# S5 output side: scan states brought into operand layout by a ScalarE copy and a round trip through DRAM, in place of VectorE and TensorE transposes

## The chip, the cores and the metric

The kernel runs on one core of one Trainium2 chip. The metric is the time of one execution on the device in microseconds; the time before is the median of three runs. TensorE (PE) multiplies matrices, VectorE (DVE) and ScalarE (ACT) do elementwise work and evacuate PSUM, GpSimd (POOL) does a little elementwise work and issues some DMAs, SyncE (SP) issues most DMAs. The 16 DMA engines of the core serve all queues.

## What is computed

Two layers on a sequence of 256 frames with 2048 channels: a gated linear attention layer (GLA) and an S5 layer, each with a modulation by a conditioning vector, a gate path and a layer norm around it. The change lies in the S5 layer, in the output side of its state space model. Cut to what matters:

```python
proj = u_in @ w_in                                  # 2048 -> 2 x 4096
u, z = jnp.split(proj, 2, axis=-1)
# 256 groups of 16 channels, 64 complex states each
bu = einsum('blgi,gpi->blgp', u_b, b)               # input side
x  = associative_scan(lam * x_prev + bu)            # over the 256 frames
y  = einsum('blgp,gip->blgi', x_r, c_re) - einsum('blgp,gip->blgi', x_i, c_im)
y  = gelu(y + d_skip * u)
y  = y * sigmoid(y @ w_glu + b_glu)
y  = (y * silu(z)) @ w_out
```

All matrices are float32; the large products are computed as three products of float32r halves (high x high, low x high, high x low), so every weight tile is split into `hi` (a ScalarE cast) and `lo` (a VectorE subtraction).

## The kernel before

Time is laid out in stages, each a loop over weight tiles of 512 KB: `v`, `q` and `z` of the GLA layer, its output product, then for S5 `su` (u), `sz` (z), `gl` (the GLU product) and the output product. A weight tile is loaded by SP (`wload`, line 136), split (`split`, lines 145 and 146) and multiplied (`st_step`, lines 180 to 182, 24 matmuls a step). The other work runs beside it: closures wait in a list `bg`, and after each weight step `pump(rate)` takes out as many as the rate says, in the order of the list. What is emitted is put in program order on each engine's queue; each engine works through its queue in order.

The S5 sequence is cut into 32 blocks of 8 frames. The state enters each block by a scan over the blocks, done on VectorE (`scan`, lines 1188 to 1190, half of the groups at a time) in the tile `sx` (partition; half, block c, part r, group n). The output of the 8 frames of a block is then, for each f (8 groups, f = 0 to 31), the sum of a product of the inputs `U` with a Toeplitz kernel `mt` and of the states at the block's start with C times the powers of lambda (`wc`).

The `sz` stage has 8 groups g of 8 weight steps. Group 0 finishes the input side. Then the list `bg` is filled with the output side, which runs beside groups 1 to 7 (56 steps) at `Y_RATE` items a step. For f = 0 to 33 the list holds:

- three scan steps of the second half of the groups, as long as there are any (30 in all, so in the first ten f);
- `cside(f)`: `cload(f + 1)` (lines 1221 and 1223: one DMA of C and powers, two of the C with its halves swapped) and `mload(f)` (line 1237), both on SP, and `cunit(f)`, the two VectorE products of lines 1070 and 1071 that make `wc`;
- `xstage(f - 1)`: the states of f are transposed by VectorE in 32 x 32 blocks out of `sx` (line 1245, tile `xT`), then by TensorE with the identity (line 1248, two transposes into PSUM, `psxs`), and copied by ScalarE to `xS` (line 1250);
- `ystage(f - 2)`: the matmuls with `mt` (line 1260) and with `xs` and `wc` (line 1263) into `psy`, a VectorE transpose (line 1266, `yt`) and the gelu on ScalarE (line 1267), which writes back into `U`.

The 126 items at 2.311 a step end within the 56 steps. `dma` is a DMA issued by SP, `wdma` one issued by GpSimd. The DRAM tile `rec` holds for each f and partition the rows C, powers of lambda and B that `cload`, `bload` (lines 1050 and 1052) and `kload` (line 1060) read; it is written by GpSimd's DMAs in the preparation (lines 613 and 628), which runs beside the GLA layer. After each group, ScalarE applies the SiLU to `sz` (line 1290).

Of the kernel before, what the change touches and what calls it, by code (L numbers as in the profile page):

```python
# [8 lines left out]
F32 = mybir.dt.float32  # L9
# [6 lines left out]
P = 128  # L16
D = 2048
E = 4096
T = 256
# [14 lines left out]
def trunk(ctx, tc, x, c, ln_g, ln_b, ada_w, ada_b, gla_w_in, gla_gate_w2, gla_gate_b, gla_norm_g,  # L34
# [3 lines left out]
    V, S, PE = nc.vector, nc.scalar, nc.tensor  # L38
# [32 lines left out]
    tp = Phase()  # L71
# [8 lines left out]
    def psx(name):  # L80
        return ax.tile([P, 512], F32, tag="ax", name=name)
# [377 lines left out]

    rec = dp.tile([P, 32, 384], F32, name="rec")

    dk = dp.tile([512, 1920], F32, name="dk")
    dxn = dp.tile([T, D], F32, name="dxn")

    l8 = cp.tile([P, 2, 2, 2, 64], F32, name="l8")
    dT = cp.tile([16, 256], F32, name="dT")
# [129 lines left out]
    def prep_pow(t):  # L598

        pw = SM["pw"]  # L600
        pd = s8t(f"pd{t}", [8, 2, 2, 64])
        for h in range(2):
            S.copy(pd[:, :, :, h, :], pw[:, :, :, t * 64:t * 64 + 64])
        lc = s8t(f"lc{t}", [16, 2, 8, 8])
        for ri in range(2):
            for nb in range(2):
                ps = psx(f"pspw{t}{ri}{nb}")
                for i in range(4):
                    n = nb * 4 + i
                    PE.transpose(ps[:, i * P:(i + 1) * P], pd[:, n, ri].rearrange("g h p -> g (h p)"), ident)  # L610
                pv = ps.rearrange("p (n f g) -> p n f g", n=4, f=16)
                S.activation(lc[:, :, ri, :, nb * 4:nb * 4 + 4].rearrange("p f g n -> p n f g"), pv, AF.Identity, scale=sgn if ri else 1.0)
        wdma(rec[:, 16 * t:16 * t + 16, 128:256], lc.rearrange("p f r g n -> p f (r g n)"))

    def to_rows(src, i_of, t, o, nm):
        got = {}

        def step(ib):
            if ib == 0:
                got["a"] = s8t("rows" + nm, [128, 16])  # L620
            a = got["a"]
            ps = psx(f"psr{nm}{ib}")
            for i in range(4):
                PE.transpose(ps[:, i * P:(i + 1) * P], i_of(src(), 4 * ib + i), ident)
            S.copy(a[:, :, 4 * ib:4 * ib + 4].rearrange("p g i -> p i g"), ps.rearrange("p (i g) -> p i g", i=4))
            if ib == 3:
                av = a.rearrange("p (f g) i -> p f (g i)", f=16)
                wdma(rec[:, 16 * t:16 * t + 16, o:o + 128], av)

        return [lambda ib=ib: step(ib) for ib in range(4)]  # L630

    def prep_b(t):
        got = {}

        def load():
            bi = s8t(f"bin{t}", [2, 64, 16])
            got["bi"] = bi
            dma(bi[:, 0], s5_b_re[0, t * P:(t + 1) * P])
            dma(bi[:, 1], s5_b_im[0, t * P:(t + 1) * P])

        def comp():
            bi = got["bi"]
            bb = s8t(f"bb{t}", [2, 64, 16])
            tm = s8t(f"bt{t}", [64, 16])
            cr = SM["cr"][:, t * 64:t * 64 + 64].unsqueeze(2).to_broadcast([P, 64, 16])
            ci = SM["ci"][:, t * 64:t * 64 + 64].unsqueeze(2).to_broadcast([P, 64, 16])
            V.tensor_tensor(bb[:, 0], bi[:, 0], cr, op=ALU.mult)
            V.tensor_tensor(tm, bi[:, 1], ci, op=ALU.mult)
            V.tensor_tensor(bb[:, 0], bb[:, 0], tm, op=ALU.subtract)
            V.tensor_tensor(bb[:, 1], bi[:, 1], cr, op=ALU.mult)  # L650
            V.tensor_tensor(tm, bi[:, 0], ci, op=ALU.mult)
            V.tensor_tensor(bb[:, 1], bb[:, 1], tm, op=ALU.add)
            got["b"] = bb.rearrange("g r p i -> g (r p) i")

        return [load], [comp] + to_rows(lambda: got["b"], lambda s, i: s[:, :, i], t, 256, f"b{t}")

    def prep_c(t):
        got = {}

        def load():  # L660
            ci = s8t(f"cin{t}", [2, 16, 64])
            got["ci"] = ci
            dma(ci[:, 0], s5_c_re[0, t * P:(t + 1) * P])
            dma(ci[:, 1], s5_c_im[0, t * P:(t + 1) * P])

        def comp():
            ci = got["ci"]
            cc = s8t(f"cc{t}", [16, 2, 64])
            S.copy(cc[:, :, 0, :], ci[:, 0])
            S.mul(cc[:, :, 1, :], ci[:, 1], -1.0)  # L670
            got["c"] = cc

        return [load], [comp] + to_rows(lambda: got["c"], lambda s, i: s[:, i].rearrange("g r p -> g (r p)"), t, 0, f"c{t}")

    (lb0, cb0), (lc0, cc0), (lb1, cb1), (lc1, cc1) = prep_b(0), prep_c(0), prep_b(1), prep_c(1)
    lam = prep_lambda()
# [9 lines left out]
    KEEP = (4, 6)  # L686
    GATE_AT = 20
    SCAN_RATE = 1.728
    Y_RATE = 2.311
    qt, kt = qk  # L690
    gl = {}

# [354 lines left out]
    def bload(f2):  # L1047

        a = tp.tile([P, 2, 384], F32, tag="rb", name=f"rb{f2}", bufs=2)
        dma(a[:, :, 0:256], rec[:, 2 * f2:2 * f2 + 2, 128:384])  # L1050
        for h in range(2):
            dma(a[64 * h:64 * h + 64, :, 256:384], rec[64 - 64 * h:128 - 64 * h, 2 * f2:2 * f2 + 2, 256:384])
        rb[f2] = a

    rc = {}
# [1 line left out]
    def kload(f2):  # L1057

        a = rc[f2] = tp.tile([P, 2, 144], F32, tag="rc", name=f"rc{f2}", bufs=2)
        dma(a, rec[:, 2 * f2:2 * f2 + 2, 0:144])  # L1060

    wb = {}

    def powmul(o, t, a0, a1, l):

        n = o.shape[2]
        bc = lambda z: z.rearrange("p (g i) -> p g i", g=8).unsqueeze(2).to_broadcast([P, 8, n, 16])
        lv = l.rearrange("p (r g n) -> p r g n", r=2, g=8)
        lq = lambda r: lv[:, r, :, :n].unsqueeze(3).to_broadcast([P, 8, n, 16])
        V.tensor_tensor(o, bc(a0), lq(0), op=ALU.mult)  # L1070
        V.tensor_tensor(t, bc(a1), lq(1), op=ALU.mult)
# [146 lines left out]

    def cload(f):
        a = tp.tile([P, 384], F32, tag="cl", name=f"cl{f}", bufs=2)  # L1220
        dma(a[:, 0:256], rec[:, f, 0:256])
        for h in range(2):
            dma(a[64 * h:64 * h + 64, 256:384], rec[64 - 64 * h:128 - 64 * h, f, 0:128])
        cl[f] = a

    def cunit(f):
        a = cl[f]
        w = [tp.tile([P, 8, 8, 16], F32, tag=f"wc{i}", name=f"wc{i}{f}", bufs=2) for i in range(2)]
        powmul(w[0], w[1], a[:, 0:128], a[:, 256:384], a[:, 128:256])
        wc[f] = w  # L1230

    kap = dk[:, :]
# [6 lines left out]

    xss = {}  # L1240

    def xstage(f):
        xt_ = tp.tile([P, 2, 4, 32], F32, tag="xt", name=f"xT{f}", bufs=1)
        n = 2 * (f % 16)
        V.transpose(xt_, sx[:, f // 16, 0:32, :, n:n + 2].rearrange("p c r b -> p b r c"))
        px = psx(f"psxs{f}")
        for b in range(2):
            PE.transpose(px[:, b * P:(b + 1) * P], xt_[:, b].rearrange("p r l -> p (r l)"), ident)
        xs = tp.tile([P, 2, 128], F32, tag="xs", name=f"xS{f}", bufs=2)
        S.copy(xs, px[:, :T].rearrange("p (b r) -> p b r", b=2))  # L1250
        xss[f] = xs

    def ystage(f):
        xs = xss[f]
        py = psx(f"psy{f}")
        U = Ut[f // 8][:, f % 8]
        for b in range(2):
            o = py[:, b * P:(b + 1) * P]
            for q in range(4):
                PE.matmul(o[32 * q:32 * q + 32], lhsT=U[:, b, 32 * q:32 * q + 32], rhs=mt[f][:, :, 2 * q + b, :], start=True, stop=False)  # L1260
            for w in wc[f]:
                for q in range(4):
                    PE.matmul(o[32 * q:32 * q + 32], lhsT=xs[:, b, 32 * q:32 * q + 32],
                              rhs=w[:, 2 * q + b].rearrange("p n i -> p (n i)"), start=False, stop=(w is wc[f][-1]))
        yt = tp.tile([P, 8, 32], F32, tag="yt", name=f"yt{f}", bufs=2)
        V.transpose(yt, py[:, :T].rearrange("p (b t i) -> p t b i", b=2, t=8))
        S.activation(U, yt.rearrange("p t c -> p (t c)").rearrange("p (b r) -> p b r", b=2), AF.Gelu_apprx_tanh)

# [7 lines left out]
    for g in range(8):  # L1276
# [14 lines left out]
        if g == 0:  # L1291
            bstep(len(bq))
            while bg:
                bg.pop(0)()
            less(mid)
            tp.close()
            tp.open("tmp2")
            cload(0)
            sc1 = [lambda cidx=cidx: scan(cidx, 1) for cidx in range(1, 31)]
            for f in range(34):  # L1300
                for _ in range(3):
                    if sc1:
                        bg.append(sc1.pop(0))
                if f < 32:
                    bg.append(lambda f=f: cside(f))
                if 1 <= f < 33:
                    bg.append(lambda f=f: xstage(f - 1))
                if f >= 2:
                    bg.append(lambda f=f: ystage(f - 2))
    while bg:  # L1310
# [149 lines left out]
```

## Time and profile before

| | us |
|---|---|
| three runs | 1847.47 (median), 1845.74, 1847.80 |
| profiled execution, first to last instruction (its span) | 1844.7 |
| `sz` beside the output side (first matmul of group 1 to the first of `gl`) | 1067.5 to 1296.3 |
| busy TensorE, VectorE, ScalarE, GpSimd over the span | 1795.5, 1422.5, 897.4, 72.7 |

For the profiled execution the span is listed and no device time of its own; the median of the runs is 2.8 us above that span. The page divides the span into 40 slices and gives each engine's busy share in tenths. "PEld" is the loading of weights into TensorE, which overlaps its matmuls. The share of DMA is that of the 16 DMA engines together. In the groups, the columns are line, engine, operation, output and input tiles, count, then busy time and mean duration in ns, then the idle time just before and what ended it. The chain of waits is the work that ended last, followed back from the end; a piece of it shows where the time itself went.

### The profile page before, as it was taken

The numbers are of one execution on the slowest core, as the hardware profiler recorded it, in microseconds if no ns is written. First come the engines' busy times: TensorE is split into PE (matmuls) and PEld (weight loads), VectorE is DVE, ScalarE is ACT, GpSimd is POOL, SyncE is SP. The second block draws the span as 40 slices with busy tenths as digits, with TensorE's granted clock in tenths as the row PEclk, the third lists the DMA queues.
The fourth block names the chain that finished last, engine by engine and source line by source line (L and its number), as shares of the span: only waits on it lengthen the run. The fifth ranks groups of instructions, "written<-read, shape, count | busy, mean of one in ns | idle before, by whom it ended". The sixth has DMA issues, their size and how long they took to land.

```text
span 1844.7 us, 33886 instructions
## 1 busy us (share of the span) xinstructions
PE 1795.5 (97%) x13619; PEld 1588.5 (86%) x13619; DVE 1422.5 (77%) x1890; ACT 897.4 (49%) x1252; POOL 72.7 (4%) x78
## 2 busy tenths in 40 slices
PE   7999999999999999999999999999999999999997
PEld 5776897899999888899999999988888888888885
DVE  4877657879989888697899689888677775557556
ACT  5433557556556333654454454545544444444332
POOL 0000000000000000002223200000000000000000
PEclk9999999999999999999999999999999999999999
DMA  9996875889889998465654477899688886668653
GB/s 343 386 333 248 294 244 164 279 261 325 291 286 317 333 353 281 163 220 158 183 151 147 139 214 222 235 246 238 224 276 264 276 271 206 191 189 325 194 184 92
DMA packets 243798, 449.48 MB, mean 244 GB/s; under 512 B 19572, under 2 KB 48942, under 8 KB 242358
## 3 DMA queue, kind: packets, MB, share of 16 engines
q1 hardware_dynamic: 239320, 436.02, 73.9%
q0 software_dynamic: 3552, 10.24, 1.8%
q8 instruction: 107, 1.75, 0.4%
q10 hardware_dynamic: 768, 1.05, 0.2%
q14 instruction: 51, 0.42, 0.1%
HBM read 432.81 MB, written 14.42 MB: 242 GB/s over the span
## 4 chain that ended last, share of the span: by engine, by line
PE 86%; DVE 8%; DMA 3%; ACT 2%; issue 2%; SPq 0%; DVEq 0%; ACTq 0%
PE gl L192 13%; PE gl L193 7%; PE op L168 6%; PE op L167 6%; PE op L169 6%; PE z L182 3%; PE z L180 3%; PE z L181 3%; PE sz L180 3%; PE v L168 3%; PE v L169 3%; PE sz L181 3%; PE sz L182 3%; PE v L167 3%; PE su L180 2%; PE su L182 2%
## 5 line engine op out<-in xcount | busy, mean ns | idle before, releaser
L146 DVE TENSOR_TENSOR logl<-wgl,higl 128x1024 fp32r<-128x1024 f32 x128 | 156.5, 1224 | 115.3 <-ACT higl L145 113.7
L145 ACT CAST higl<-wgl 128x1024 fp32r<-128x1024 f32 x128 | 134.4, 1051 | 172.2 <-PE gl L192 167.9
L192 PE MATMUL gl<-yb,higl 128*128 128x512 f32 x512 | 179.6, 395 | 0.0
L192 PE MATMUL gl<-yp,higl 128*128 128x512 f32 x512 | 179.3, 395 | 0.1
L145 ACT CAST hio<-wo 128x1024 fp32r<-128x1024 f32 x95 | 100.2, 1055 | 155.3 <-PE op L169 127.3
L146 DVE TENSOR_TENSOR loo<-wo,hio 128x1024 fp32r<-128x1024 f32 x95 | 116.2, 1225 | 67.2 <-ACT hio L145 63.7
L315 DVE SCALAR_TENSOR_TENSOR acc<-wa,cs,acc 128x512 f32<-128x512 f32 x217 | 162.2, 748 | 4.8 <-DMA wa<-in_ada_w 2.1
L180 PE MATMUL su<-u1h,hisu 128*128 128x256 f32 x512 | 153.5, 301 | 1.9 <-DVE vv L1108 1.9
L180 PE MATMUL sz<-u1h,hisz 128*128 128x256 f32 x512 | 149.7, 292 | 1.2 <-ACT zs L1290 1.2
L180 PE MATMUL z<-u0h,hiz 128*128 128x256 f32 x512 | 148.7, 290 | 0.0
L182 PE MATMUL su<-u1h,losu 128*128 128x256 f32 x512 | 145.7, 286 | 0.4 <-DVE losu L146 0.4
L181 PE MATMUL su<-u1l,hisu 128*128 128x256 f32 x512 | 145.8, 285 | 0.0
L182 PE MATMUL z<-u0h,loz 128*128 128x256 f32 x512 | 144.9, 283 | 0.6 <-DVE loz L146 0.6
L182 PE MATMUL sz<-u1h,losz 128*128 128x256 f32 x512 | 144.9, 283 | 0.0
L181 PE MATMUL sz<-u1l,hisz 128*128 128x256 f32 x512 | 144.7, 283 | 0.0
L181 PE MATMUL z<-u0l,hiz 128*128 128x256 f32 x512 | 144.7, 283 | 0.0
L193 PE MATMUL gl<-yb,logl 128*128 128x256 f32 x512 | 143.4, 280 | 0.0
L193 PE MATMUL gl<-yp,logl 128*128 128x256 f32 x512 | 142.0, 280 | 0.0
L145 ACT CAST hisz<-wsz 128x1024 fp32r<-128x1024 f32 x64 | 66.9, 1051 | 107.2 <-PE sz L181 55.1
L192 PEld LDWEIGHTS gl<-yb,higl 128*128 128x128 f32 x512 | 96.0, 188 | 22.6
L192 PEld LDWEIGHTS gl<-yp,higl 128*128 128x128 f32 x512 | 95.8, 188 | 22.6 <-issue 0.6
L145 ACT CAST hisu<-wsu 128x1024 fp32r<-128x1024 f32 x64 | 66.7, 1050 | 95.1 <-PE su L181 70.6
(322 smaller groups left out, 5019.8 us busy)
## 6 DMA issues: line engine op xcount, KB each, us to landing
wgl<-in_s_w_glu SPq DMA_DIRECT2D x128, 512.0 KB, 4.7
wa<-in_ada_w SPq DMA_DIRECT2D x116, 512.0 KB, 5.1
wv<-in_gla_w_in SPq DMA_DIRECT2D x64, 512.0 KB, 6.1
wz<-in_gla_w_in SPq DMA_DIRECT2D x64, 512.0 KB, 5.2
wsu<-in_s_w_in SPq DMA_DIRECT2D x64, 512.0 KB, 3.7
wsz<-in_s_w_in SPq DMA_DIRECT2D x64, 512.0 KB, 4.3
wo<-in_s_w_out SPq DMA_DIRECT2D x64, 512.0 KB, 4.5
a<-in_ada_w SPq DMA_DIRECT2D x31, 1024.0 KB, 10.7
```

The source lines that it names most:

```text
L145: S.copy(hi, w)
L146: last_lo[0] = V.tensor_tensor(lo, w, hi.bitcast(F32), op=ALU.subtract).ins
L167: PE.matmul(banks[tt], lhsT=uh, rhs=hi[:, kk, :], start=(k == first), stop=False)
L168: PE.matmul(banks[tt], lhsT=uh, rhs=lo[:, kk, :], start=False, stop=False)
L169: last_mm[0] = PE.matmul(banks[tt], lhsT=ul, rhs=hi[:, kk, :], start=False, stop=(k == last)).ins
L180: PE.matmul(o, lhsT=wh, rhs=u.hi(k), start=(k == first), stop=False)
L181: PE.matmul(o, lhsT=wh, rhs=u.lo(k), start=False, stop=False)
L182: last_mm[0] = PE.matmul(o, lhsT=wl, rhs=u.hi(k), start=False, stop=(k == last)).ins
L192: PE.matmul(banks[f], lhsT=hi[:, kk, fs], rhs=u.both(k), start=(k == 0), stop=False)
L193: PE.matmul(banks[f][:, :T], lhsT=lo[:, kk, fs], rhs=u.hi(k), start=False, stop=(k == last))
L315: V.scalar_tensor_tensor(acc[0], w[:, kk, :], cs[:, k:k + 1], acc[0], op0=ALU.mult, op1=ALU.add)
```

## The change

- `xstage` is replaced by two functions. `xwrite(f)` lets ScalarE copy the states of f out of `sx` into a dense tile `xt_` (one buffer) in the order part r, group b, block c, and GpSimd's queue writes it as 128 rows of 1 KB to a new DRAM tile `dx`. `xread(f)` reads them back on the same queue so that the partitions hold (state l, part r) and the free axis the quarter q: 512 pieces of 256 B. `xs` has three buffers.
- The partitions of `xs` are now in another order, (l r) in place of (r l), and `wc` must have the same. `cload` therefore reads its rows in that order, and in one DMA of 1536 B a row: `rec` is widened to 512 and also holds C with its halves swapped, which two further GpSimd DMAs for each half of the groups write in the preparation. Offsets in `bload` and `kload` move along.
- The lhsT of line 1263 is `xs[:, q, b]`.
- `yt` has one buffer in place of two.
- In the list, `xwrite(f + 1)` (for f = 0 also `xwrite(0)`) and `xread(f)` stand between `cside(f)` and `ystage(f - 2)`. The list has 158 items, and `Y_RATE` is 2.9.

```diff
-    rec = dp.tile([P, 32, 384], F32, name="rec")
+    rec = dp.tile([P, 32, 512], F32, name="rec")
+    dx = dp.tile([32, P, 256], F32, name="dx")
...
                 wdma(rec[:, 16 * t:16 * t + 16, o:o + 128], av)
+                if o == 128:
+                    for h in range(2):
+                        wdma(rec[64 * h:64 * h + 64, 16 * t:16 * t + 16, 0:128], av[64 - 64 * h:128 - 64 * h])
...
-    Y_RATE = 2.311
+    Y_RATE = 2.9
...
     def cload(f):
         a = tp.tile([P, 384], F32, tag="cl", name=f"cl{f}", bufs=2)
-        dma(a[:, 0:256], rec[:, f, 0:256])
-        for h in range(2):
-            dma(a[64 * h:64 * h + 64, 256:384], rec[64 - 64 * h:128 - 64 * h, f, 0:128])
+        dma(a, rec[:, f, 0:384].rearrange("(r l) x -> l r x", r=4))
         cl[f] = a
...
-        powmul(w[0], w[1], a[:, 0:128], a[:, 256:384], a[:, 128:256])
+        powmul(w[0], w[1], a[:, 128:256], a[:, 0:128], a[:, 256:384])
...
-    def xstage(f):
-        xt_ = tp.tile([P, 2, 4, 32], F32, tag="xt", name=f"xT{f}", bufs=1)
+    def xwrite(f):
+        xt_ = tp.tile([P, 4, 2, 32], F32, tag="xt", name=f"xT{f}", bufs=1)
         n = 2 * (f % 16)
-        V.transpose(xt_, sx[:, f // 16, 0:32, :, n:n + 2].rearrange("p c r b -> p b r c"))
-        px = psx(f"psxs{f}")
-        for b in range(2):
-            PE.transpose(px[:, b * P:(b + 1) * P], xt_[:, b].rearrange("p r l -> p (r l)"), ident)
-        xs = tp.tile([P, 2, 128], F32, tag="xs", name=f"xS{f}", bufs=2)
-        S.copy(xs, px[:, :T].rearrange("p (b r) -> p b r", b=2))
-        xss[f] = xs
+        S.copy(xt_, sx[:, f // 16, 0:32, :, n:n + 2].rearrange("p c r b -> p r b c"))
+        wdma(dx[f], xt_.rearrange("p r b c -> p (r b c)"))
+
+    def xread(f):
+        xs = xss[f] = tp.tile([P, 4, 2, 32], F32, tag="xs", name=f"xS{f}", bufs=3)
+        wdma(xs.rearrange("p q b c -> p q (b c)"), dx[f].rearrange("(q l) (r x) -> (l r) q x", q=4, r=4))
...
-                    PE.matmul(o[32 * q:32 * q + 32], lhsT=xs[:, b, 32 * q:32 * q + 32],
+                    PE.matmul(o[32 * q:32 * q + 32], lhsT=xs[:, q, b],
...
-        yt = tp.tile([P, 8, 32], F32, tag="yt", name=f"yt{f}", bufs=2)
+        yt = tp.tile([P, 8, 32], F32, tag="yt", name=f"yt{f}", bufs=1)
...
-                if 1 <= f < 33:
-                    bg.append(lambda f=f: xstage(f - 1))
+                for i in range(0 if f == 0 else f + 1, min(f + 2, 32)):
+                    bg.append(lambda i=i: xwrite(i))
+                if f < 32:
+                    bg.append(lambda f=f: xread(f))
                 if f >= 2:
                     bg.append(lambda f=f: ystage(f - 2))
```

More of the change, by code (lines that the diff above doesn't have):

```diff
@@ L612, in prep_pow @@
                 S.activation(lc[:, :, ri, :, nb * 4:nb * 4 + 4].rearrange("p f g n -> p n f g"), pv, AF.Identity, scale=sgn if ri else 1.0)
-        wdma(rec[:, 16 * t:16 * t + 16, 128:256], lc.rearrange("p f r g n -> p f (r g n)"))
+        wdma(rec[:, 16 * t:16 * t + 16, 256:384], lc.rearrange("p f r g n -> p f (r g n)"))
     def to_rows(src, i_of, t, o, nm):
@@ L653, in comp @@
             got["b"] = bb.rearrange("g r p i -> g (r p) i")
-        return [load], [comp] + to_rows(lambda: got["b"], lambda s, i: s[:, :, i], t, 256, f"b{t}")
+        return [load], [comp] + to_rows(lambda: got["b"], lambda s, i: s[:, :, i], t, 384, f"b{t}")
     def prep_c(t):
@@ L671, in comp @@
             got["c"] = cc
-        return [load], [comp] + to_rows(lambda: got["c"], lambda s, i: s[:, i].rearrange("g r p -> g (r p)"), t, 0, f"c{t}")
+        return [load], [comp] + to_rows(lambda: got["c"], lambda s, i: s[:, i].rearrange("g r p -> g (r p)"), t, 128, f"c{t}")
     (lb0, cb0), (lc0, cc0), (lb1, cb1), (lc1, cc1) = prep_b(0), prep_c(0), prep_b(1), prep_c(1)
@@ L1049, in bload @@
         a = tp.tile([P, 2, 384], F32, tag="rb", name=f"rb{f2}", bufs=2)
-        dma(a[:, :, 0:256], rec[:, 2 * f2:2 * f2 + 2, 128:384])
+        dma(a[:, :, 0:256], rec[:, 2 * f2:2 * f2 + 2, 256:512])
         for h in range(2):
-            dma(a[64 * h:64 * h + 64, :, 256:384], rec[64 - 64 * h:128 - 64 * h, 2 * f2:2 * f2 + 2, 256:384])
+            dma(a[64 * h:64 * h + 64, :, 256:384], rec[64 - 64 * h:128 - 64 * h, 2 * f2:2 * f2 + 2, 384:512])
         rb[f2] = a
@@ L1059, in kload @@
         a = rc[f2] = tp.tile([P, 2, 144], F32, tag="rc", name=f"rc{f2}", bufs=2)
-        dma(a, rec[:, 2 * f2:2 * f2 + 2, 0:144])
+        dma(a, rec[:, 2 * f2:2 * f2 + 2, 128:272])
     wb = {}
```

## The prediction

> **What bounds the kernel now.** I read the page first, then the engines' busy time in stretches, then the stretch that the change touches by its groups, its chain of waits, its waits and its DMA.
>
> ```profile
> PE 1795.5 (97%) x13619; PEld 1588.5 (86%) x13619; DVE 1422.5 (77%) x1890; ACT 897.4 (49%) x1252; POOL 72.7 (4%) x78
> DMA  9996875889889998465654477899688886668653
> ```
>
> Over the whole span TensorE is the bound, but the DMA digits rise to 9 in places. The edited code runs in the seven groups of `sz` that follow group 0, from 1067.5 us to the first `gl` matmul at 1296.3 us. By stretches (columns: length, then busy time of PE, PEld, DVE, ACT, POOL, granted clock, DMA share, GB/s):
>
> ```profile
> 1067.50:1152.50 85.00, 83.76 (x939) 80.91 (x938) 81.25 (x148) 40.94 (x59) 0.00 (x0) 1.00 0.78 223
> 1152.50:1210.00 57.50, 57.13 (x824) 53.44 (x823) 50.35 (x55) 29.37 (x47) 0.00 (x0) 1.00 0.91 241
> 1210.00:1265.00 55.00, 50.89 (x733) 47.20 (x731) 44.40 (x48) 28.11 (x43) 0.00 (x0) 1.00 1.00 238
> 1265.00:1290.00 25.00, 24.26 (x375) 22.49 (x376) 23.47 (x30) 14.25 (x27) 0.00 (x0) 1.00 0.98 247
> 1290.00:1296.30 6.30, 6.30 (x88) 5.95 (x87) 6.30 (x12) 5.93 (x9) 0.00 (x0) 1.00 0.37 107
> 1067.50:1296.30 228.80, 222.33 (x2951) 209.99 (x2950) 205.78 (x288) 118.60 (x182) 0.00 (x0) 1.00 0.88 230
> 1296.30:1664.00 367.70, 367.63 (x2088) 320.31 (x2087) 243.29 (x289) 178.05 (x227) 0.00 (x0) 1.00 0.75 241
> ```
>
> The stage has two halves. In the first 85 us (the scan of the second half runs beside it) VectorE is nearly as full as TensorE and the DMA engines are free 22% of the time. From 1152.5 us on there is no scan, so more f pass per weight step, and DMA is at 0.91, 1.00 and 0.98. The groups of the stretch (from 1066 to 1300 us) that the change names, and steps of the chain of waits (start, length):
>
> ```profile
> L1245 DVE STREAM_TRANSPOSE xT<-sx 128x256 f32<-128x256 f32 x32 | 20.1, 627 | 1.2 <-PE psxs L1248 0.9
> L1248 PE MATMUL psxs<-ident,xT 128*128 128x128 f32 x64 | 12.3, 274 | 1.2 <-DVE xT L1245 1.2
> L1250 ACT COPY xS<-psxs 128x256 f32<-128x256 f32 x32 | 11.5, 361 | 2.0 <-PE psxs L1248 2.0
> L1267 ACT ACTIVATE U<-yt 128x256 f32<-128x256 f32 x32 | 13.3, 416 | 6.5 <-DVE yt L1266 6.4
> ```
> ```profile
> 1060.11 0.12 PE sz L182
> ...
> 1123.61 0.39 ACT zs L1290
> ...
> 1182.11 0.22 PE psxs L1248 x2
> 1182.33 0.36 PE psy L1260 x8
> 1182.68 0.44 PE psy L1263 x16
> 1183.12 0.22 PE psy L1260 x8
> 1183.34 0.44 PE psy L1263 x16
> ```
> ```profile
> 1214.00 9.58 DMA wsz<-in_s_w_in
> ...
> 1231.71 8.37 DMA mt<-dk
> ...
> 1252.65 9.60 DMA cl<-rec
> ```
>
> Matmuls overlap, so the 274 ns of a transpose is not its price; the chain is. One weight step is 24 x 0.12 = 2.88 us of TensorE, one `psy` block 0.36 + 0.44 + 0.22 + 0.44 = 1.46 us, the pair of transposes 0.22 us. 56 steps, 32 blocks and 32 pairs make 161.3 + 46.7 + 7.0 = 215.0 of the 228.8 us: TensorE sets the pace. But the three long DMA pieces of the chain all lie between 1214 and 1263 us, where the share is 1.00: there DMA is already level with TensorE. The waits from 1152.5 to 1296.3 us say the same (waiter, releaser, total us, times, longest):
>
> ```profile
> DVE wc L1070 <- DMA cl<-rec: 7.4, 3, 2.6
> PE psy L1260 <- DMA mt<-dk: 3.9, 3, 1.9
> ACT hisz L145 <- DMA wsz<-in_s_w_in: 3.5, 1, 3.5
> PE psxs L1248 <- DVE xT L1245: 1.2, 2, 0.8
> ```
>
> **The change part by part.** The span is 1844.7 us and the median of the three runs 1847.47, 2.8 us more; I add the differences to the median.
>
> *Removed.* The pair of transposes: 32 x 0.22 = 7.0 us of TensorE, all on its path, and its wait of 1.2 us for `xT`. VectorE's transpose: 32 x 0.627 = 20.1 us, beside TensorE except where the first half's VectorE queue delays a ScalarE release (0.39 us piece at 1123.61 ends such a wait; I allow 1.5 us). Where these stalls go, weights or `mt` are late next.
>
> *ScalarE.* The copy from PSUM (0.361 us) goes, a copy from strided SBUF comes. The nearest row of that size out of SBUF is `U`, 0.416 us; a price from 0.36 to the 0.63 of the strided VectorE read of the same columns gives 0 to +9 us of ScalarE in all; I take 0.42, +2 us. ScalarE is busy 118.6 of 228.8 us: hidden. The copy now also waits for the write of the copy before it (one buffer), with casts and the gelu queued behind; that is the last rival.
>
> *The queue of SP.* Three issues of `cl` per f become one, bytes unchanged; less waiting on SP, nothing where its buffers are the limit:
>
> ```profile
> SPq L1221 <- DVE yt L1266: 55.9, 28, 4.2
> ```
>
> I count 0 to -2 us, and take 0. `yt` with one buffer, `xs` with three, and the wider rows of `rec` for `rb` and `rc` (same pieces) cost nothing by the same rows.
>
> *The new DMAs*, on GpSimd's queue, which is empty in this stage (POOL 0.00 above). Per f 128 KB are written in rows of 1 KB and 128 KB read back in 512 pieces of 256 B. Rows that price them: all DMA of the stretch from 1067 to 1297 us, a GpSimd write of 1 MB nearly by itself (293 to 299 us, 6 us), small pieces (106.9 to 108.2 us, 1.3 us, with that window's packet count), and GpSimd's queue over the whole span (columns: packets, MB, share of 16 engines):
>
> ```profile
> q1 hardware_dynamic: 29624, 52.56, 86.7%
> ```
> ```profile
> q0 software_dynamic: 258, 1.04, 68.3%
> ```
> ```profile
> DMA packets 636, 0.31 MB, mean 235 GB/s; under 512 B 548, under 2 KB 550, under 8 KB 636
> ...
> q1 hardware_dynamic: 636, 0.31, 80.4%
> ```
> ```profile
> q0 software_dynamic: 3552, 10.24, 1.8%
> ```
>
> The stage pays 0.867 x 230 / 52.56 = 3.79 us of all 16 engines per MB, the write 0.683 x 6 / 1.04 = 3.94. So the write is 0.131 MB x 3.94 = 0.52 us. The read is 0.50 at the stage's rate, or 512 x (0.804 x 1.3 x 16 / 636 = 26 ns) / 16 = 0.84 by the small pieces. The cheapest row, all of q0 over the span (0.018 x 1844.7 / 10.24 = 3.24 us per MB), gives 0.42 for each. Ends 0.85 and 1.36 us per f; I take 1.05, near the stage's own rate.
>
> The Trainium skill, page "DMA: Bandwidth & Descriptors", section Specifications, puts the least transfer for full rate at 512 B and says that below it the engine reads, modifies and writes. The small pieces' window moves its 0.31 MB at 0.804 x 1.3 / 0.31 = 3.4 us per MB, not slower than the stage, so this trace does not bear the rule out; were the read at half rate by it (1.0 us), I estimate about 10 us more than my sum.
>
> *The order.* Before, the first ten f hold 57 of 126 items, after 69 of 158; at 2.311 and 2.9 a step that is 24.7 and 23.8 steps, then 31.3 and 32.2.
> - First part: TensorE before 24.7 x 2.88 + 8 x 1.46 + 9 x 0.22 = 84.8 us (85 measured); after 23.8 x 2.88 + 11.7 = 80.2. DMA there: 0.78 x 85 = 66.3, less 0.9 load, plus ten f at 1.05 = 75, still under 80. VectorE 81.3 - 9 x 0.63 - 1 = 75. So 80.2: a gain of 5.
> - Second part: TensorE would need 32.2 x 2.88 + 24 x 1.46 = 127.8 us. DMA before: 52.3 + 55.0 + 24.5 + 2.3 = 134.1 us (shares by lengths). After: +0.9 load of 0.524 MB (1.8), +21.5 f at 1.05 (22.6). Of the eight prefetched `gl` loads (2.0 us each), half can slip, since the `gl` stage has a share of 0.75: -8. That leaves 150.5 us, and at the 0.98 of the stretch 1265 to 1290, 153.6 us.
> - Sum 233.8 against 228.8: +5.0 us. With 0.85 per f it is +0.6; with 1.36 and 0.96 filled, +15.
>
> *Preparation.* Four more writes of 512 KB: 2.1 x 3.94 = 8.3 us of DMA near 293 and 348 us, where there is room:
>
> ```profile
> 280.00:380.00 100.00, 97.77 (x521) 79.79 (x520) 81.65 (x100) 63.00 (x80) 3.46 (x3) 1.00 0.73 234
> ```
>
> 27 us of the hundred are free, so 0; if that cover were gone, up to 8.3.
>
> **The rivals.**
> *DMA yields* (other side). An engine that is busy at 1.00 moves 238 GB/s here, while 293 to 299 us shows 1.04 MB in 4.1 us, 254, and the first digits of the page are also 9: the packets of this stage may be stretched by one another, and small ones slip in between. Then TensorE stays the bound: -7.0 - 1.2 - 1.5 = -9.7, 1838 us. It begins to pay once an f costs DMA under 0.82 us ((148.6 x 0.98 - 127.9) / 21.5, with 148.6 = 228.8 - 80.2 and 127.9 = 134.1 + 1.8 - 8), and reaches 1838 only if the packets of weights and `mt` shrink too. Against it: three DMA waits of 8 to 10 us in the chain already.
> *Even.* All eight `gl` loads slip and are made up later: 8 us less, 1845 to 1847 us. For it: share 0.75 after 1296.3; against: `gl` then starts without weights.
> *The write's landing closes a loop.* Copy, issue, landing, next copy share one buffer, and ScalarE's casts stand behind it. Rows of such writes:
>
> ```profile
> L1162 POOL DMA_DIRECT2D dk<-ks x32 | 19.7, 616 | 5.1 <-POOL ks L1159 5.1
> ```
> ```profile
> dk<-ks POOLq DMA_DIRECT2D x32, 64.0 KB, 3.3
> ```
>
> 0.42 + 0.62 + 3.3 = 4.3 us against 4/2.9 x 2.88 + 1.46 = 5.4 us per f: it fits, but only up to a landing of 4.4 us; at 6.5 a step would be 7.5 us where my DMA bound makes 153.6 / 22 = 7.0, some 11 to 13 us more, 1865 us.
>
> **How the numbers follow.** DMA becomes the bound: 0.40, own range 1848 to 1863, likeliest 1852.5. DMA yields: 0.30, 1834 to 1843. Even: 0.22. The loop: 0.08, around 1865. About 0.2% (3.7 us) can be told from no change here. Faster 0.30, same 0.23 (Even and a little of the forecast's lower end), slower 0.47. The range 1836 to 1864 leaves out the lowest tenth and the loop's upper half.
>
> **What would show it.** Right: no `psxs` rows, `sz` and `psy` at 0.12 and 1.46 us, the stage some 5 us longer; the first part near 80 us; then DMA at 1.00 up to the end of `sz`, and TensorE or the casts waiting for `wsz`, `mt` or `cl`. Wrong: a DMA share under 0.95 in the second part, or an f costing DMA under 0.8 us with TensorE busy throughout; or ScalarE standing before the new copy, with the DMA engines idle.

## The result, and the profile after

The changed kernel takes 1900.94 us (median of four runs, 1895.65 to 1909.69) beside 1846.61 us for the kernel before (four runs, 1844.6 to 1847.8). The ratio is 1.0297, with a 95% interval of 1.0272 to 1.0322: 3% slower. The forecast of 1852.5 us had the sign, and a tenth of the size; the time lies far above its range. The profiled execution has a span of 1898.0 us, 53.3 above that of before.

From the page of the changed kernel, the busy times, the clock and the DMA digits of the 40 slices, and GpSimd's DMA queue:

```profile
PE 1806.3 (95%) x13555; PEld 1596.8 (84%) x13555; DVE 1406.9 (74%) x1858; ACT 900.8 (47%) x1248; POOL 117.5 (6%) x146
...
PEclk9999999999999999999999988899999999999998
DMA  9996876879889996565554666799778887668662
...
q0 software_dynamic: 7200, 20.73, 3.7%
```

The transposes are gone (64 fewer TensorE instructions, 32 fewer on VectorE), the new traffic is there (10.5 MB more on GpSimd's queue: 8.4 of x, 2.1 of the rows in the preparation), but TensorE's share falls to 95%, the clock's digits fall to 8, and the DMA digits in the edited stage are 6, 6 and 7 where they were 7, 7 and 8, before the 9 of its end. For most of the stage neither TensorE nor DMA is the bound any more.

Where the time went is read from three points of the trace: the first `sz` matmul, the first `gl` matmul and, between them, the last scan step. The first `sz` comes at 1041.2 us (before: 1036.0), the first `gl` at 1350.3 (1296.1), and what follows takes as long as it did. So 5.2 us are lost ahead of the stage and 49.0 in it. By stretches of the stage (length, busy PE, PEld, DVE, ACT, POOL, granted clock, DMA share, GB/s):

```profile
1067.00:1150.00 83.00, 65.61 (x635) 62.39 (x634) 55.17 (x97) 36.49 (x52) 15.97 (x26) 0.91 0.68 204
1150.00:1200.00 50.00, 45.00 (x549) 42.66 (x549) 36.59 (x54) 24.02 (x35) 7.03 (x11) 0.90 0.76 214
1200.00:1250.00 50.00, 37.60 (x486) 34.74 (x485) 26.82 (x28) 20.42 (x31) 10.35 (x18) 0.83 0.75 217
1250.00:1300.00 50.00, 47.16 (x668) 44.23 (x666) 41.45 (x44) 21.24 (x31) 6.33 (x9) 1.00 1.04 264
...
1067.00:1350.00 283.00, 237.58 (x2931) 223.33 (x2931) 196.18 (x261) 126.47 (x182) 43.42 (x67) 0.91 0.79 219
```

In the first three rows no engine is full: TensorE is busy 148 of 183 us, ScalarE 81, the DMA share is 0.68 to 0.76. Something waits in a circle. In the fourth row the picture is suddenly the one that was forecast: DMA at 1.04, TensorE nearly full, clock 1.00. The last copy of states starts at 1246.8 us; the circle ends there. TensorE's idle time in the stage is 283.0 - 237.6 = 45.4 us, where it was 228.8 - 222.3 = 6.5.

The waits of 1067 to 1360 us name the circle (waiter, releaser, total us, times, longest):

```profile
POOL dx L1248 <- ACT xT L1247: 103.5, 27, 5.8
ACT xT L1247 <- DMA dx<-xT: 81.3, 26, 6.2
POOL xS L1252 <- PE psy L1264: 75.0, 17, 8.6
DVE losz L146 <- ACT hisz L145: 62.3, 33, 6.8
...
PE sz L180 <- ACT zs L1291: 25.8, 4, 9.2
```

ScalarE stands 81.3 us before the new copy, waiting for the landing of the write before it, 3.1 us at each of 26 copies. Behind ScalarE stands VectorE's half of the split (62.3 us where it was 8.1), and TensorE, because the SiLU that frees its PSUM bank is also in ScalarE's queue. A part of ScalarE's timeline (start, length, instruction, and in brackets the idle time before it) shows what is queued behind what:

```profile
1085.38 0.65 ACT L1247 COPY xT<-sx 128x256 f32<-128x256 f32 x1 [3.51 <-DMA dx<-xT]
1085.93 1.04 ACT L145 CAST hisz<-wsz 128x1024 fp32r<-128x1024 f32 x1
1091.89 0.62 ACT L1247 COPY xT<-sx 128x256 f32<-128x256 f32 x1 [4.92 <-DMA dx<-xT]
1092.42 1.04 ACT L145 CAST hisz<-wsz 128x1024 fp32r<-128x1024 f32 x1
1095.67 0.65 ACT L1247 COPY xT<-sx 128x256 f32<-128x256 f32 x1 [2.21 <-DMA dx<-xT]
1096.23 1.04 ACT L145 CAST hisz<-wsz 128x1024 fp32r<-128x1024 f32 x1
```

In this part there is one copy between every two casts, so one for each weight step. That isn't the order of the list, by which the description of the kernel before and the prediction went: in the trace nine copies stand on ScalarE's queue ahead of the first gelu, where the list has four. The copies come in two runs of 16, from 1073.8 to 1148.0 us with 15 casts and from 1171.8 to 1247.5 us with 13; between the runs they wait for the scan of the second half. Within a run the states are ready, and nothing but the buffer holds the copies back. A weight step is 2.88 us of TensorE; the circle takes longer, 4.9 and 5.0 us from copy to copy on the average of the two runs, as the chain of waits through the same place shows (start, length, what):

```profile
1081.24 4.06 DMA dx<-xT
1085.30 0.28 issue
1085.58 0.74 POOL xS L1252
1086.32 5.49 DMA dx<-xT
1091.82 0.28 issue
1092.10 0.74 POOL xS L1252
1092.84 2.75 DMA dx<-xT
```

From write to write that is 5.1 and 6.5 us, for a copy that stands in the way of one cast. The chain is drawn through the read, which waited for the same landing on GpSimd's queue, but the copy runs at the same time: it starts at 1085.38 us, ends at 1086.03, and the write follows 0.29 us later, just as it does where no read stands between (a copy ends at 1096.32, the write starts at 1096.61). So the circle is the landing, the copy and about 0.4 us of hand-over between them.

### The profile page after: what moved, and what is told of

Same layout as the page of the kernel before. It is cut to its first block, busy times and chain, and to the rows that moved or that the text cites. A ratio compares the mean times of both kernels' runs of the same rounds, so it can differ in the third digit from the quotient of the medians.

```text
span 1898.0 us, 33748 instructions
## 1 busy us (share of the span) xinstructions
PE 1806.3 (95%) x13555; PEld 1596.8 (84%) x13555; DVE 1406.9 (74%) x1858; ACT 900.8 (47%) x1248; POOL 117.5 (6%) x146
## 3 DMA queue, kind: packets, MB, share of 16 engines
q10 hardware_dynamic: 768, 1.05, 0.2%
## 4 chain that ended last, share of the span: by engine, by line
PE 79%; DVE 7%; DMA 6%; issue 5%; ACT 3%; POOL 1%; SPq 0%; DVEq 0%; ACTq 0%; POOLq 0%
PE gl L192 12%; PE gl L193 6%; PE op L168 6%; PE op L169 6%; PE op L167 6%; PE z L182 3%; PE z L180 3%; PE z L181 3%; PE v L168 3%; PE v L169 3%; PE v L167 2%; PE sz L180 2%; DMA dx<-xT 2%; PE su L180 2%; PE su L182 2%
## 5 line engine op out<-in xcount | busy, mean ns | idle before, releaser
L180 PE MATMUL sz<-u1h,hisz 128*128 128x256 f32 x512 | 155.3, 303 | 31.6 <-ACT zs L1291 25.8
L182 PE MATMUL sz<-u1h,losz 128*128 128x256 f32 x512 | 150.7, 294 | 3.2 <-DVE losz L146 3.0
L181 PE MATMUL sz<-u1l,hisz 128*128 128x256 f32 x512 | 150.0, 293 | 0.0
L180 PEld LDWEIGHTS sz<-u1h,hisz 128*128 128x128 f32 x512 | 103.4, 202 | 39.4 <-ACT zs L1291 26.7
L146 DVE TENSOR_TENSOR losz<-wsz,hisz 128x1024 fp32r<-128x1024 f32 x64 | 77.8, 1220 | 75.8 <-ACT hisz L145 75.6
```

The costliest lines, as they stand in the source:

```text
L146: last_lo[0] = V.tensor_tensor(lo, w, hi.bitcast(F32), op=ALU.subtract).ins
L180: PE.matmul(o, lhsT=wh, rhs=u.hi(k), start=(k == first), stop=False)
L181: PE.matmul(o, lhsT=wh, rhs=u.lo(k), start=False, stop=False)
L182: last_mm[0] = PE.matmul(o, lhsT=wl, rhs=u.hi(k), start=False, stop=(k == last)).ins
```

## The experiments

The theory after the result was the circle through the one buffer of `xt`, tightened by the order on ScalarE's queue. Its rivals were the x traffic alone (the forecast's own mechanism, only larger), the side edits, and GpSimd's queue as the link that is slow. Stage lengths below run from the first `sz` to the first `gl`: 260.1 us before, 309.1 after.

| kernel | median us | ratio to before (interval) | stage us |
|---|---|---|---|
| after | 1900.94 | 1.0297 (1.0272 to 1.0322) | 309.1 |
| after, copy ordered behind the gelu of f - 4 | 1874.92 | 1.0148 (1.0125 to 1.0171) | 284.4 |
| the same, write issued by ScalarE | 1875.31 | 1.0145 (1.0110 to 1.0179) | 285.2 |
| after, two buffers | 1883.64 | 1.0205 (1.0176 to 1.0233) | 291.7 |
| after, eight buffers | 1868.12 | 1.0111 (1.0078 to 1.0144) | 275.9 |
| eight buffers, copy behind the gelu of f - 4 | 1892.20 | 1.0235 (1.0205 to 1.0265) | 296.4 |
| eight buffers, copy behind the gelu of f - 8 | 1863.75 | 1.0099 (1.0075 to 1.0123) | 268.0 |
| before + side edits | 1852.13 | 1.0025 (1.0010 to 1.0040) | 261.2 |
| before + traffic tied to its own operand | 1874.78 | 1.0146 (1.0122 to 1.0170) | 279.0 |
| before + reads in 256 B pieces (writes fell ahead of the stage) | 1858.63 | 1.0069 (1.0044 to 1.0093) | 270.0 |
| before + reads in 1 KB rows (the same) | 1854.10 | 1.0034 (1.0019 to 1.0048) | 263.9 |
| before + writes and reads, tied to nothing | 1855.82 | 1.0045 (1.0029 to 1.0062) | 270.5 |

**The order alone.** The copies are spread: each stands on ScalarE's queue behind the gelu of four f before.

```diff
+        with tc.issue_after(gelu[f - 4]) if f >= 4 else nullcontext():
+            S.copy(xt_, sx[...])
```

> The changed kernel, with one edge more: in ScalarE's queue the copy of f stands behind the gelu of f - 4 instead of where the planner put it (it had put 16 copies ahead of the fourth gelu and all 32 ahead of the fifteenth). Traffic, buffers and items are the same. Theory Q: the 81 us that ScalarE waits for landings fall below 20, the waits of TensorE for zs go, the clock stays at 1.00, and the time falls by 35 to 55 us to 1845 to 1866. Theory T: the traffic is the same, so the time falls by no more than 10 us. A third theory, B (the single buffer itself, whatever the order): each copy still waits for the landing of the one before, and the time falls by less than 20 us.

The time falls by 26 us, the stage by 24.7: between what was expected if the order were all and what was expected if it were the buffer. The wait is shorter but still there:

```profile
ACT xT L1248 <- DMA dx<-xT: 58.1, 19, 8.1
```

So about half of the loss goes with the order; with one buffer ScalarE still stands before 19 of the 32 copies.

**Two buffers.** There was room for a second buffer of `xt` only with one fewer of `xs`.

```diff
-tag="xt", name=f"xT{f}", bufs=1)
+tag="xt", name=f"xT{f}", bufs=2)
-tag="xs", name=f"xS{f}", bufs=3)
+tag="xs", name=f"xS{f}", bufs=2)
```

> The changed kernel with two buffers for the dense copy and two instead of three for xs (there is no room for one more of both). Theory B: a copy waits for the landing of the one before the last, the time falls by 25 us or more. Theory Q: the planner sets the copies still earlier when it has two buffers (16 ahead of the first gelu), and on GpSimd's queue writes stand ahead of reads and reads behind the matmuls that free xs; so no gain beyond 15 us, or a loss. Theory T: unchanged within 10 us.

A gain of 17 us for both edits together, again between the expected values; what the missing buffer of `xs` costs in it isn't separated. With more room the copies moved even further ahead (sixteen stand before the first gelu), and the wait was halved, not removed:

```profile
POOL xS L1252 <- PE psy L1264: 128.8, 22, 9.5
...
ACT xT L1247 <- DMA dx<-xT: 42.1, 19, 5.5
```

**The issuing queue.** The copy behind the gelu of f - 4, and the write issued from ScalarE's own queue, so that no read on GpSimd's queue stands between.

```diff
-        wdma(dx[f], xt_...)
+        S.dma_start(dx[f], xt_...)
```

> The changed kernel, copies pinned behind the gelu of f - 4, one buffer, and the write issued from ScalarE's own DMA queue, so that no write stands behind a read that waits for a free xs on GpSimd's queue. Theory B with the queue of GpSimd as the link (landing seen by ScalarE = wait in that queue + landing): the pinned kernel's 58 us of waits fall to below 25 and the time to 1850 to 1862. If the landing itself is the price: ScalarE waits as long, and its issues cost it some 0.6 us per f more, 1870 to 1880.

1875.31 beside 1874.92 us: nothing gained. The wait for the landing is 48.2 us at 17 copies, so GpSimd's queue isn't the slow link of the ordered version; the landing is.

**Eight buffers.** The copies of eight f share one 8 KB tile, each in its own eighth.

```diff
+        if f % 8 == 0:
+            xq[0] = s8t(f"xT{f}", [8, 4, 2, 32])
+        xt_ = xq[0][:, f % 8]
```

> The changed kernel with eight buffers for the copies and the planner's own order (it puts the copies of eight f one behind the other). Theory B (landing behind one buffer is the price): ScalarE's waits nearly go, 1845 to 1860, as with the pin. Theory Q (order is the price): still 20 us above before, since copies ahead of casts and writes ahead of reads stay.

33 us of the 54 come back by the buffer alone, and ScalarE no longer waits for a landing before any copy. Still, the time is above the 1845 to 1860 us that were expected if the one buffer were the whole price. The waits of 1042 to 1330 us that are left:

```profile
POOL xS L1254 <- PE psy L1266: 148.1, 25, 11.1
...
DVE wc L1074 <- DMA cl<-rec: 26.9, 11, 4.5
...
PE psy L1263 <- DMA mt<-dk: 22.5, 12, 5.2
```

The first is GpSimd's queue, which stands before a read until the matmuls free an operand; TensorE isn't seen waiting for these reads here. The others are waits for loads, as forecast for the second part.

**Eight buffers and the order, f - 4.** Both edits together.

```diff
+        xt_ = xq[0][:, f % 8]
+        with tc.issue_after(gelu[f - 4]) if f >= 4 else nullcontext():
+            S.copy(xt_, sx[...])
```

> The changed kernel with both causes on ScalarE taken away: the copies stand behind the gelu of f - 4, and they have eight buffers (an 8 KB tile for eight f) instead of one, so that none waits for the landing before it. Traffic and side edits stay. Theory Q+B: ScalarE's wait for landings goes from 58 us (pinned alone) to near 0; TensorE loses the transposes; 1838 to 1856 with the 4 to 6 us of the side edits. Theory T: the traffic stays, so it stays where the pinned kernel was, 1865 to 1875.

This was a miss: 1838 to 1856 us were expected, and 1892.20 is 24 us worse than the eight buffers alone. A write whose copy waits for a gelu stands on GpSimd's queue ahead of a read that `psy` needs, and the operand comes late:

```profile
POOL dx L1251 <- ACT xT L1250: 30.0, 10, 7.2
...
PE psy L1267 <- DMA xS<-dx: 19.0, 7, 4.8
```

An order that helps one queue was a new wait on the next.

**Eight buffers and the order, f - 8.** The same with more slack.

```diff
+        with tc.issue_after(gelu[f - 8]) if f >= 8 else nullcontext():
```

> The changed kernel with eight buffers for the copies and each copy behind the gelu of f - 8. With the edge at f - 4 it was slower (1892) than with no edge (1868): the write of f + 4 stood ahead of the read of f + 1 on GpSimd's queue, and waited for the gelu of f, so the operand came late (TensorE waited 19 us for it). If that is why, the looser edge gives 1855 to 1870; if eight buffers with any edge are bad, 1880 or more.

1863.75 us, the lowest of the changed family, though its interval overlaps that of the eight buffers alone, and still slower than the kernel before: 37 of the 54 us are gone, and the stage is 7.9 us longer than before instead of 49.0. Its first stretches now look like those the forecast assumed:

```profile
1042.00:1125.00 83.00, 82.37 (x916) 79.36 (x914) 62.82 (x105) 42.63 (x65) 21.11 (x30) 1.00 0.71 213
1125.00:1200.00 75.00, 73.58 (x989) 69.57 (x988) 62.87 (x83) 43.84 (x63) 15.30 (x25) 1.00 0.98 272
1200.00:1260.00 60.00, 53.58 (x743) 50.13 (x741) 44.46 (x45) 26.56 (x40) 12.36 (x19) 0.97 1.02 272
1260.00:1310.00 50.00, 42.75 (x598) 39.57 (x599) 37.42 (x45) 27.82 (x41) 4.30 (x6) 0.90 0.81 214
```

TensorE is full while the scan lasts, then DMA is at 0.98 and 1.02 and TensorE has gaps. The last stretch is another matter: DMA is at 0.81, and TensorE is busy 43 of 50 us. The chain of waits runs from 1213.8 to 1260.6 us through the issues on GpSimd's queue, and ends in the landing of the last write, for which ScalarE waits once more, ahead of the SiLU that TensorE needs:

```profile
ACT L1294 <- DMA dx<-xT: 5.0, 1, 5.0
```

Between the issues lie 1.6 to 6.0 us for which the profile names no cause. The SiLU's output and the copies take their tiles from the same pool of 8 KB tiles, so the wait of 5.0 us probably came in with the eight buffers; no run leaves it out.

**The side edits alone.** The kernel before with the wide `rec`, its four extra writes and the single `cload`.

```diff
-    rec = dp.tile([P, 32, 384], F32, name="rec")
+    rec = dp.tile([P, 32, 512], F32, name="rec")
+                if o == 128:
+                    for h in range(2):
+                        wdma(rec[64 * h:..., 0:128], av[64 - 64 * h:...])
-        dma(a[:, 0:256], rec[:, f, 0:256])
-        for h in range(2):
-            dma(a[64 * h:64 * h + 64, 256:384], rec[...])
+        dma(a, rec[:, f, 0:384])
```

> The kernel before with the side edits alone: rec of 512 columns with the swapped C, four more writes of 512 KB in the preparation, one DMA of 1536 B a row in place of three for each f (in the old partition order). The stages before su began 5 us later in the changed kernel. If the four writes cost that, 2 to 6 us longer than before; if it is another order of the planner there, 0. The single DMA itself: 0 to -3 us in all theories.

Ratio 1.0025: 4.6 us, nearly all ahead of the stage, which itself has 261.2 us. So the single `cload` is worth nothing that can be told, as forecast, and the writes in the preparation aren't free.

**The traffic alone, first try.** The kernel before, with the write of 128 KB from its operand `xS` and a read of 128 KB in 256 B pieces that nothing uses.

```diff
         xss[f] = xs
+        wdma(dx[f], xs.rearrange("p b r -> p (b r)"))
...
+        junk = tp.tile([P, 4, 64], F32, tag="jk", ...)
+        wdma(junk, dx[f].rearrange("(q l) (r x) -> (l r) q x", q=4, r=4))
```

> The kernel before with the DMA traffic of the change and nothing else: after ScalarE has made xS of f, GpSimd writes it as 128 rows of 1 KB to a DRAM tile, and before the output matmuls of f it reads 512 pieces of 256 B into a tile that nobody uses; the transposes stay, yt has one buffer to make room. Theory T (traffic: the DMA engines are the limit of the second part, as predicted): 8 MB more at about 3.8 us per MB, some 32 us of all engines where some 20 are free, so 10 to 15 us longer than before (1857 to 1862), DMA share 0.98 or more from the stage's middle on. Theory Q (queue order: the copies that stand early in ScalarE's queue, each behind the landing of the write before, hold the casts and the SiLU up): no copy waits for a landing here, so within 5 us of before, 1843 to 1852.

28 us, more than the 10 to 15 that were expected for traffic, and the waits say why: `xS` has two buffers, its writer is ScalarE, and so the kernel before got the same kind of circle.

```profile
ACT xS L1251 <- DMA dx<-xS: 45.7, 14, 8.2
```

As a price of the traffic it can't be used; as a test of the circle it says much, since besides the traffic nothing else of the change is in that kernel. Its stage is 18.9 us longer than before, where the same traffic tied to nothing (below) makes 10.4.

**The traffic tied to nothing.** The writes come from a constant tile. In the first two kernels they were then issued far ahead of the stage (168 to 192 us), so those price the reads alone, in 256 B pieces and in rows of 1 KB.

```diff
+        wdma(dx[f], l8.rearrange("p a b c d -> p (a b c d)")[:, 0:256])
+        junk = tp.tile([P, 4, 64], F32, tag="jk", ...)
+        wdma(junk, dx[f].rearrange("(q l) (r x) -> (l r) q x", q=4, r=4))   # 1 KB: wdma(junk, dx[f])
```

> The kernel before with the change's DMA traffic, now without any tie to the compute engines: for each f GpSimd writes 128 rows of 1 KB from a constant tile to a DRAM tile and reads them back as 512 pieces of 256 B into a tile that nobody uses. (In the first try the write's source was xS, and ScalarE waited 46 us for its landings: it had the loop in it that it was to leave out.) Theory T (traffic alone): as that try, 1860 or more. Theory Q/B (the waits tied to the landings cost the time): within 6 us of before, 1842 to 1853; each percent of DMA that it adds shows as share, not as time.

> The kernel before with 32 reads of 128 KB from the DRAM tile into an unused tile beside the output side, as 128 rows of 1 KB each; the 32 writes go out early, in the GLA stage at some 170 to 190 us, where the planner also put them in the earlier try with free traffic, so that try had only the reads of 256 B pieces in the stage (16 us of all engines, 0.51 us a read, and the stage 10 us longer). If pieces of 256 B are slow, the 1 KB reads cost about half (0.25 us a read) and the stage is some 5 us longer than before; if the bytes count, 0.4 to 0.5 us a read and again 8 to 10 us longer; total 1850 to 1859.

GpSimd's queue in the stage (packets, MB, share of 16 engines), 256 B pieces over 239 us, then 1 KB rows over 240 us:

```profile
q0 software_dynamic: 1536, 4.20, 6.8%
```
```profile
q0 software_dynamic: 1632, 4.33, 6.4%
```

That is 0.068 x 239 / 4.20 = 3.87 us of all engines per MB beside 0.064 x 240 / 4.33 = 3.55 (two other writes of 64 KB are in the second figure). The lengths of the stage differ more: 9.9 us longer than before with the pieces of 256 B, 3.8 with the rows of 1 KB, which is what was expected if short pieces are slow, while the DMA time per MB is what was expected if only the bytes count. The intervals of the two ratios overlap, and each stage is read from one trace, so this stays open. In the third kernel the write of each f stands on GpSimd's queue behind the read of the f before, so that both are in the stage:

```diff
+        with tc.issue_after(rd[f - 1]) if f else nullcontext():
+            wdma(dx[f], l8...[:, 0:256])
```

> The kernel before with both halves of the traffic in the stage, free of the compute engines: each write (from a constant tile) is issued behind the read before it on GpSimd's queue. Theory T with the prediction's price of 1.05 us per f: 32 x 1.05 = 34 us of all engines, the DMA share of the stage's second part at 1.00, and the stage 15 to 22 us longer than before (reads alone were 10), total 1860 to 1868. If a write that is free costs little, as the reads' cost came from something else than engine time: as with the reads alone, 1856 to 1860.

The two DMA queues over 1070 to 1310 us:

```profile
q1 hardware_dynamic: 29971, 53.23, 82.6%
q0 software_dynamic: 3024, 8.26, 12.8%
```

0.128 x 240 / 32 = 0.96 us for an f, in a stage that is 10.4 us longer than before; the whole kernel is 1.0045 of before, 8.3 us. With a price for every byte 15 to 22 us in the stage were expected; with the writes added it is hardly longer than with the reads of 256 B alone.

## Why the prediction was wrong, and where it was right

**The step that failed** is "0.42 + 0.62 + 3.3 = 4.3 us against ... 5.4 us per f: it fits", with "ScalarE is busy 118.6 of 228.8 us: hidden". The mechanism is that of the rival named last, with a chance of 0.08 and 1865 us; the sign that the prediction gave for it, ScalarE standing before the new copy with the DMA engines idle, is what the trace shows, at DMA shares of 0.68 to 0.76. Three things were wrong in the step.

- The yardstick. 5.4 us per f holds if the copies are spread like the f. In two runs of 16 they came about one for each weight step, every 2.88 us of TensorE. A circle of 4.3 us could not fit that, while the 4.9 to 5.0 us that were measured from copy to copy would still have passed the test against 5.4: it is the test that failed, more than the size.
- The circle. The copy took 0.65 us and not 0.42 (it reads strided elements out of `sx`; the dense row of `U` was the wrong neighbour, the strided VectorE read of 0.63 the right one), and the hand-overs of 0.4 us were left out. The 0.62 us of the issue were counted twice, since the landing is counted from the start of the issue (the write issued at 1081.24 us has landed 4.06 us later). The landing was taken from writes of 64 KB, as one figure; for the 128 KB here it is longer and not constant:

```profile
L1247 ACT COPY xT<-sx x32: 622/656/684, 1073.8 to 1246.8; 128x256 f32<-128x256 f32 x32
...
DMA to landing us min/median/max: 2.0/3.8/5.8
```

- The price. 11 to 13 us were reckoned as a longer step of the DMA-bound second part. But what stands is ScalarE, and behind it the casts and the SiLU of a stage that TensorE paces; its low busy share hid nothing of that. The loss was 22 us already in the first part.

The Trainium skill, page "DMA: Bandwidth & Descriptors", section Anatomy of one DMA, gives about 2 us of fixed cost for a DMA, most of it the confirmation that the last byte has landed. The least landing here, 2.0 us with the moving of 128 KB in it, is about that; the median of 3.8, and of 6.6 in the version with eight buffers ordered by f - 8, shows that beside other DMA traffic it is a floor and no price.

**The sum behind the likeliest case came out near**, once the circle is opened, but not all of its terms did. The scan marks the two parts of the stage. Its first rows before, after, with eight buffers and f - 8, and with the traffic tied to nothing (last column: first and last start):

```profile
L1188 DVE TENSOR_TENSOR sca<-sx,l x30: 373/424/428, 1068.2 to 1143.8; 128x256 f32<-128x256 f32 x30
```
```profile
L1192 DVE TENSOR_TENSOR sca<-sx,l x30: 382/424/427, 1073.4 to 1170.6; 128x256 f32<-128x256 f32 x30
```
```profile
L1192 DVE TENSOR_TENSOR sca<-sx,l x30: 383/426/428, 1074.7 to 1147.8; 128x256 f32<-128x256 f32 x30
```
```profile
L1189 DVE TENSOR_TENSOR sca<-sx,l x30: 381/424/427, 1069.4 to 1144.8; 128x256 f32<-128x256 f32 x30
```

| | scan, first to last | last scan to first `gl` |
|---|---|---|
| before | 75.6 | 152.3 |
| after | 97.2 | 179.7 |
| eight buffers, f - 8 | 73.1 | 162.6 |
| traffic tied to nothing | 75.4 | 161.0 |

- First part: forecast 80.2 for 84.8 or 85 us, a gain of 5. With eight buffers and f - 8 it is 2.5, half of that.
- Second part: forecast 153.6 for 143.8 us, +9.8. Measured +10.3, and +8.7 with the traffic alone. That the numbers meet is in part luck. In the version with eight buffers and f - 8, DMA is at 0.98 and 1.02 only up to 1260 us; then comes the stretch at 0.81. The 8 us that were taken off because loads of `gl` can slip aren't borne out: six of them are issued ahead of the first `gl` matmul before, after and in both versions of this table, and without that term the sum is 158.5 / 0.98 = 161.7, +18. The reads of 256 B alone make the second part 161.5 us, +9.2, with half of the bytes: the sum adds up by bytes, and these runs do not. The rival "Even", that all of the `gl` loads slip, goes with the same count.
- Traffic: 1.05 us per f taken, 0.96 measured, within the ends of 0.85 and 1.36.
- "DMA yields" (0.30) did not come true at the point that it named: with 8.26 MB more in the stage the packets of weights and `mt` took 0.826 x 240 / 53.23 = 3.72 us per MB beside 3.79 before. They shrink by 2%, and the stage is 10.4 us longer. But its premise has something in it: a DMA share of 1.00 went with 238 GB/s before, and 1.02 with 272 in the version with eight buffers and f - 8. So a share near 1 doesn't show that no more could be moved.
- The rule of the 512 B, from the same page of the Trainium skill, on which the estimate of 10 us more hung: pieces of 256 B took 3.87 us per MB beside 3.55 for rows of 1 KB, 9% more and not twice as much. So the DMA time of these reads doesn't show the rule's price; the lengths of the stage (9.9 us longer than before, beside 3.8) would allow one, and the runs don't decide it.

**The preparation was not free.** Taken at 0, with 8.3 us "if that cover were gone": the side edits alone cost 4.6 us, and the changed kernel starts its stage 5.2 us later. The last two of the added writes are issued at 352.0 and 352.8 us in the changed kernel, where the first weights of the GLA layer's `z` are loaded (from 350.9 us). ScalarE waits once for these weights, 7.8 to 8.4 us in each of the eight kernels that have the writes and 3.1 to 4.9 in the five others; before, and in the changed kernel:

```profile
ACT hiz L145 <- DMA wz<-in_gla_w_in: 4.1, 1, 4.1
```
```profile
ACT hiz L145 <- DMA wz<-in_gla_w_in: 7.8, 1, 7.8
```

A DMA share of 0.73 over a hundred microseconds didn't mean that this moment had room.

**The account.** Of 53.3 us in the profiles, 5.2 lie ahead of the stage and 49.0 in it. 41.1 of these go with the buffer and the order (309.1 to 268.0); 7.9 stay, and the traffic alone makes 10.4. By the ratios, 1.0099 for the best changed version is 0.0029 more than the side edits and the traffic together (0.0025 + 0.0045), about what the intervals leave. But the transposes that it no longer has should have made it faster, by the 2.5 us measured in the first part at least, so some 8 us of it have no run of their own; the chain through GpSimd's queue is where its trace points.

What stays open: how much of the loss is the lower clock. The three stretches in which the circle runs have 0.91, 0.90 and 0.83 with TensorE busy 79%, 90% and 75%, and the one after it 1.00 at 94%. The Trainium skill, page "TensorE: Matmul & The Clock Gate", section Part 1: The HAM clock gate, says that the clock is set by how busy TensorE has lately been; these rows agree in the main, though the stretches with 79% and 90% have nearly the same clock. No run holds the gaps and changes the clock, so its share isn't separated. Which of the landings late in the second part (`mt`, `cl`) costs how much isn't either.

## What to carry to other kernels

A DMA out of a tile with one buffer makes the engine that fills the tile wait for the landing, and with it everything that stands behind on its queue; a low busy share of that engine says nothing about this. Compare the circle (copy, issue, landing, whatever is issued in between) with the spacing at which the copies will really stand on the queue, not with the rate at which their results are used, and look at whose work is next behind them. When the result is far from the forecast, open the circle first: here the forecast's sum could only be judged in the version with eight buffers and with the traffic tied to nothing. And when a total then agrees, look at its terms one by one before calling it right.

## What the runs showed of the hardware

- A write of 128 KB to DRAM landed after 2.0 to 5.8 us (median 3.8) in the changed kernel, though the DMA share there was 0.68 to 0.76; a load of 512 KB (`mt`) took 9.0 us at the median in the kernel with a DMA share of 0.96.
- ScalarE took 0.656 us to copy 128 x 256 float32 out of strided columns, and 0.414 us for a gelu of as many dense ones.
- Reads of 128 KB in 256 B pieces and in 1 KB rows differed by 9% in DMA time per MB (3.87 and 3.55 us).
- The DMA engines moved 238 GB/s at a share of 1.00 before (1210 to 1265 us), and 272 GB/s at 1.02 in the version with eight buffers and f - 8 (1200 to 1260 us).
